# Block compression in two passes of fp32r, the causal mask moved into a scan, dummy transposes at the start, and a new plan of the order

## The chip, the core and the metric

One core of one Trainium2 chip runs the whole program. Its engines are PE (TensorE, matrix products), DVE (VectorE), ACT (ScalarE) and POOL (GpSimd); SP (SyncE) issues the transfers. The time is device microseconds of one execution, given as the median of several. A profile is one execution of its own.

## What is computed

One layer of a transformer on 1024 tokens of width 1024, in fp32. After a norm and an input projection, four mixers run: (a) attention over compressed blocks, over all keys and over a window of 512, gated; (b) a short convolution; (c) stick-breaking attention; (d) dilated attention. A norm by groups, the output projection, a second norm and a gated feed-forward block follow. The two pieces that the change touches:

```python
def compress_tokens(t, pe, w1, w2):        # for keys, then for values
    idx = jnp.arange(n_cmp)[:, None] * 16 + jnp.arange(32)[None, :]     # n_cmp = 63
    blocks = (t[:, idx] + pe).reshape(b, n_cmp, 32 * 64)
    return jax.nn.gelu(blocks @ w1) @ w2                                # 2048 -> 256 -> 64

def chunk(args):                           # stick-breaking attention, 4 heads
    z = jnp.einsum('bhqd,bhsd->bhqs', qi, k) * (hd ** -0.5)
    past = key_pos[None, :] < t[:, None]
    neg_log_keep = jnp.where(past, jax.nn.softplus(z), 0.0)
    between = lax.cumsum(neg_log_keep, axis=3, reverse=True) - neg_log_keep
    attn = jnp.where(past, jnp.exp(jax.nn.log_sigmoid(z) - between), 0.0)
```

## The kernel before

**Stages.** All of it is one function, `hybrid`. `x` is loaded in eight tiles of 128 tokens, normed, transposed on PE (`norm_transpose`, L189) and kept as a high and a low part in `XH`, `XL`. Most products are three PE passes over such pairs in the fp32r format (`mm3`, L234 to L236: high by high, high by low, low by high). Each weight tile of 256 KB is loaded into one of three buffers `raw` and split by `split` (L104 on ACT writes `whi`, L105 on POOL subtracts and writes `wlo`) into a ring of twelve buffers `whl`. First come the projections for mixer (a): `wA2` (268 columns), `kv` (the tokens to be compressed) and `wa` (the queries q, eight token tiles of 24 products each, called the q products below). Then the mixers run in the sequence of `ORDER`; then output projection and feed-forward, the larger part of the time, in which PE mostly sees one product of 512 columns after the other.

**The compression (L447 to L491).** It runs once for keys and once for values, z = 0 and 1. DVE adds the position term to the 63 overlapping blocks (L451, output `St`). `w1` comes in four loads of 512 KB straight into big buffers `St`, unsplit. For each of 16 positions and two halves of the 256 hidden units PE multiplies in plain fp32, with 63 moving columns (L459); the profile counts two records for each such product, 64 for each z. Then GELU is spelled out on ACT and DVE (L463 to L470, tiles `hT` and `ge`), a small weight `w2t` is loaded (L472) and PE makes the second product (L475). `hT`, `ge` and `w2t` come from the ring `S2` of ten buffers, of which the split q weights hold eight until the last q product; so `w2t` can be loaded only when `ge` has been read for the last time, at L470.

**The mask of (c).** `attn_stick` walks over pairs of query tiles. `qk_pair` makes two products per head (L501, L503); for the chunk with the diagonal a third product (L507) adds a tile `tri`, which holds -1e30 at and above the diagonal. ACT computes the softplus in three steps, DVE sums it from the right in a scan (L781, multiplier: a broadcast one), and `car` carries the sum to the next chunk (L786).

**What sets the order.** The program is traced twice. First `make_plan` lists every instruction with an estimated duration and lets each engine take the ready instruction of smallest index less lead; the table `LEADS` holds a lead for each engine and tile name, and rings hand out buffers in program order. The second time, `fix_order` pins every engine and SP to the order so found, up to the last product stage. Each engine then works through its list strictly in order, whatever waits.

Of the kernel before, what the change touches and what calls it, by code (L numbers as in the profile page):

```python
# [9 lines left out]
F32 = mybir.dt.float32  # L10
F32R = mybir.dt.float32r
# [13 lines left out]
WARM = 0  # L25
# [23 lines left out]
def hybrid(ctx, tc, pools, x, gmix, wa1, wa2, wkv, wcv, wd, wc, bgate, gcols, pe, w1, w2,  # L49
# [397 lines left out]
    for z, src in ((0, KK), (1, VV)):  # L447
        BL = Stile()
        bv = BL[:, :16 * 63].rearrange("p (l n) -> p l n", n=63)
# [12 lines left out]
        for j in range(2):  # L462
            nc.scalar.activation(hT[:, j * NBLK:(j + 1) * NBLK], ps[j][:, :NBLK], AF.Copy)  # L463
# [32 lines left out]
    def qk_pair(Q, K, qt, c0, n, diag=None, Z=None):  # L496
# [3 lines left out]
        for h in range(2):  # L500
            nc.tensor.matmul(ps[h][:, :n], Q[h][:, qc], K[h][:, kc_], start=True, stop=False)  # L501
            q2 = Q[h][:, qc] if Z is None else Z[:, h, :]
            nc.tensor.matmul(ps[h][:, :n], q2, K[2][:, kc_], start=False, stop=diag is None)  # L503
# [247 lines left out]
    def diag_mask():  # L751
        tri = sm.tile([128, 384], F32R, tag="wct", bufs=1, name="tri")
        t0 = S2("tri0")
        nc.gpsimd.memset(t0, 0.0)
        nc.gpsimd.affine_select(t0[:, 128:256], t0[:, 128:256], pattern=[[-1, 128]],
                                compare_op=OP.is_gt, fill=-BIG, base=0, channel_multiplier=1)
        nc.vector.tensor_copy(tri, t0[:, :384])
        return tri

    def attn_stick(hp, Q, K, V):  # L760
        for qp in range(NT // 2):
# [3 lines left out]
            for ci in range(qp // 2, -1, -1):  # L765
                for j in range(2):
# [4 lines left out]
                    ps = qk_pair(Q, K, qt, c0, max(256, w), w - 128 if diag else None, Z[j])  # L771
# [1053 lines left out]
```

## Time and profile before

| | us |
|---|---|
| median of 3 runs | 1329.57 (1325.78 to 1329.8) |
| the profiled execution's own time | 1334.16 |
| its span in the trace | 1332.4 |
| PE busy | 1297.2 (97% of the span) |
| DVE, ACT, POOL busy | 1025.5, 734.3, 597.9 |
| mean granted clock of PE over the recorded stretches | 0.988 |

The span is the time from the first to the last instruction; the rest of the execution's time lies around it. PE is the only engine that is nearly always busy, so a microsecond is gained where PE has less to do or waits less. A product's record is longer than the step from its start to the next one's start, because products are pipelined: costs are read from steps. The granted clock is the share of 2.4 GHz that PE was given in a stretch; 0.50 is 1.2 GHz.

### The profile page before, as it was taken

The page shows a single profiled execution, that of the slowest core. Times are in us where ns is not written, and L with a number is a line of the kernel's source. Part 1 is how long each engine was busy: PE and PEld are TensorE (multiplying, and loading weights), DVE is VectorE, ACT ScalarE, POOL GpSimd, SP SyncE. Part 2 cuts the span into 40 slices and gives each one's busy share as a digit, 9 for nine tenths or more (in the row PEclk, how much of TensorE's full clock was granted, in tenths as well). Part 3 has the DMA queues.
Part 4 walks back from the last instruction along what each step waited for, and adds up shares of the span by engine and source line. Part 5 has one row for each costly group of instructions (what it writes and reads, how often), then busy time and mean ns, then how long its engine had stood idle before and what let it go on. Part 6 is the DMA issues. An engine that isn't in the chain of part 4 may idle for free.

```text
span 1332.4 us, 20691 instructions
## 1 busy us (share of the span) xinstructions
PE 1297.2 (97%) x7101; PEld 1108.7 (83%) x7101; DVE 1025.5 (77%) x1985; ACT 734.3 (55%) x1643; POOL 597.9 (45%) x462
## 2 busy tenths in 40 slices
PE   6999999999999999899989999999999999999998
PEld 6898889989888878799968888888888887887886
DVE  5538889988896789788678898777775877499863
ACT  5427778877877888687655233323333335523440
POOL 4424356651312043433783445454443544464755
PEclk9989999999999999899999999999999999999999
DMA  6330012121312024424363544233232239762434
GB/s 223 129 113 1 9 45 72 41 64 26 104 49 58 15 68 144 152 84 139 128 217 135 182 161 163 96 119 119 87 111 79 87 119 328 266 200 76 141 92 155
DMA packets 89402, 153.07 MB, mean 115 GB/s; under 512 B 10001, under 2 KB 35601, under 8 KB 89297
## 3 DMA queue, kind: packets, MB, share of 16 engines
q1 hardware_dynamic: 88736, 149.92, 34.5%
q0 software_dynamic: 560, 1.84, 0.4%
q8 instruction: 56, 0.92, 0.3%
q14 instruction: 50, 0.40, 0.1%
HBM read 111.08 MB, written 36.44 MB: 111 GB/s over the span
## 4 chain that ended last, share of the span: by engine, by line
PE 85%; DVE 6%; DMA 3%; issue 2%; ACT 2%; POOL 1%; SPq 0%; DVEq 0%; POOLq 0%; ACTq 0%
PE PRp L234 10%; PE PRp L235 10%; PE PRp L236 10%; PE PRp L1048 4%; PE PRp L1047 4%; PE PRp L1046 4%; PE Op L568 3%; PE Op L569 3%; PE SPp L501 2%; PE Tp L1047 2%; PE SPp L1048 2%; PE SPp L1047 2%; PE Tp L1048 2%; PE SPp L1046 2%; PE Tp L1046 2%; PE SPp L503 2%
## 5 line engine op out<-in xcount | busy, mean ns | idle before, releaser
L105 POOL TENSOR_TENSOR wlo<-raw,whi 128x512 fp32r<-128x512 f32 x86 | 118.1, 1382 | 154.0 <-ACT whi L104 105.0
L1035 POOL TENSOR_TENSOR fw<-fraw,fw 128x512 fp32r<-128x512 f32 x50 | 72.9, 1458 | 139.2 <-ACT fw L1034 134.2
L541 DVE TENSOR_TENSOR ptl<-Tp,pth 128x256 fp32r<-128x256 f32 (+1 forms) x204 | 105.6, 534 | 25.3 <-ACT pth L540 23.5
L1105 DVE TENSOR_TENSOR fw<-sraw,fw 128x512 fp32r<-128x512 f32 x73 | 89.3, 1240 | 34.1 <-ACT fw L1104 33.9
L1034 ACT ACTIVATE fw<-fs 128x512 fp32r<-128x512 f32 x88 | 52.6, 629 | 113.5 <-DVE fs L1025 82.4
L540 ACT ACTIVATE pth<-Tp 128x256 fp32r<-128x256 f32 (+1 forms) x204 | 92.0, 471 | 33.9 <-PE Tp L562 25.3
L1105 POOL TENSOR_TENSOR hw<-bB,hw 128x512 fp32r<-128x512 f32 x55 | 80.0, 1467 | 49.6 <-ACT hw L1104 49.0
L234 PE MATMUL PRp<-XH,whi 128*128 128x512 f32 x224 | 90.5, 404 | 0.0
L236 PE MATMUL PRp<-XH,wlo 128*128 128x512 f32 x224 | 89.7, 400 | 0.0
L235 PE MATMUL PRp<-XL,whi 128*128 128x512 f32 x224 | 89.6, 400 | 0.0
L650 POOL TENSOR_SCALAR S<-S,ll 128x256 f32<-128x256 f32 (+3 forms) x48 | 60.2, 1260 | 54.2 <-DVE ll L647 26.9
L1035 DVE TENSOR_TENSOR fw<-fs,fw 128x512 fp32r<-128x512 f32 x88 | 76.7, 906 | 6.6 <-ACT fw L1034 6.6
L1034 ACT ACTIVATE fw<-fraw 128x512 fp32r<-128x512 f32 x50 | 31.4, 627 | 82.7 <-DMA fraw<-in_wup_dram 27.4
L236 PE MATMUL PRp<-whi,ML 128*128 128x256 f32 (+1 forms) x248 | 72.2, 295 | 2.3 <-DVE ML L814 2.3
L234 PE MATMUL PRp<-whi,MH 128*128 128x256 f32 (+1 forms) x248 | 72.6, 294 | 0.2 <-ACT MH L813 0.2
L235 PE MATMUL PRp<-wlo,MH 128*128 128x256 f32 (+1 forms) x248 | 72.2, 292 | 0.0
L1104 ACT ACTIVATE hw<-bB 128x512 fp32r<-128x512 f32 x62 | 38.9, 628 | 55.7 <-PE Op L236 20.4
L562 PE MATMUL Tp<-ident,S 128*128 128x128 f32 x292 | 68.1, 273 | 0.6 <-DVE S L748 0.4
L104 ACT ACTIVATE whi<-raw 128x512 fp32r<-128x512 f32 x86 | 53.0, 618 | 27.7 <-DMA raw<-in_wcv_dram 11.5
L560 PE MATMUL Tp<-ident,S 128*128 128x128 f32 x260 | 65.2, 272 | 0.0
L1104 ACT ACTIVATE fw<-sraw 128x512 fp32r<-128x512 f32 x73 | 45.3, 624 | 23.1 <-DMA sraw<-hS 13.5
L642 ACT ACTIVATE S<-S,mm 128x384 f32<-128x384 f32 (+3 forms) x96 | 55.7, 583 | 3.6 <-DVE mm L533 3.3
(469 smaller groups left out, 4619.8 us busy)
## 6 DMA issues: line engine op xcount, KB each, us to landing
fraw<-in_wgate_dram SPq DMA_DIRECT2D x22, 512.0 KB, 4.2
fraw<-in_wup_dram SPq DMA_DIRECT2D x22, 512.0 KB, 4.2
bB<-in_wdown_dram SPq DMA_DIRECT2D x44, 256.0 KB, 4.9
sraw<-hS SPq DMA_DIRECT2D x44, 256.0 KB, 2.7
raw<-in_wout_dram SPq DMA_DIRECT2D x30, 256.0 KB, 2.8
hS<-s SPq DMA_DIRECT2D x30, 256.0 KB, 2.2
sraw<-hA SPq DMA_DIRECT2D x29, 256.0 KB, 3.9
xt<-in_x_dram SPq DMA_DIRECT2D x8, 512.0 KB, 9.4
```

Of the source, the lines that this page charges most:

```text
L105: (lo or nc.gpsimd).tensor_tensor(dst_lo, raw, f(dst_hi), op=OP.subtract)
L234: nc.tensor.matmul(ps, a[0], b[0], start=first, stop=False)
L235: nc.tensor.matmul(ps, a[0], b[1], start=False, stop=False)
L236: nc.tensor.matmul(ps, a[1], b[0], start=False, stop=last)
L540: nc.scalar.activation(ph[:rows, c0:c1], tp[:rows, c0:c1], AF.Copy)
L541: nc.vector.tensor_tensor(pl[:rows, c0:c1], tp[:rows, c0:c1], f(ph[:rows, c0:c1]), op=OP.subtract)
L1035: eng.tensor_tensor(wt[:, 1, :], a, f(wt[:, 0, :]), op=OP.subtract)
L1046: nc.tensor.matmul(ps, wt[:, 0, c], bh[:, k, :], start=k == 0, stop=False)
L1047: nc.tensor.matmul(ps, wt[:, 0, c], bl[:, k, :], start=False, stop=False)
L1048: nc.tensor.matmul(ps, wt[:, 1, c], bh[:, k, :], start=False, stop=k == 3)
L1104: nc.scalar.activation(wt[:, 0, :], raw, AF.Copy)
L1105: eng.tensor_tensor(wt[:, 1, :], raw, f(wt[:, 0, :]), op=OP.subtract)
```

## The change

1. **Compression.** The blocks are split into a high and a low part side by side, `bhl` (128 columns: 63 high, a zero, 63 low, a zero), in a buffer of the ring `V`, which has two (the other holds `VA`, so `bhl` of z = 1 waits for the products of z = 0). `w1` comes in 16 loads of 256 KB through `raw` and `split`; the low part is subtracted on DVE for every other load. `bhl` becomes the stationary operand, and each position has two fp32r products of 256 columns (L464, L465): 64 in all, where 64 plain fp32 products with 128 records stood. Their result lies the other way round, so it is copied out (`hs`), transposed on PE (two transposes for each z) and the high and the low half are added on DVE before GELU.
2. **Mask.** The third product per head of the diagonal chunk (32 in all) goes. A tile `keep` of ones with a zero on the diagonal, in the ring `W`, is the scan's multiplier there, and the scan starts from 1e30 instead of 0: from the right it stays at 1e30 until the zero wipes it out. One carry in a special case is multiplied by a column of `keep`.
3. **Start.** `WARM = 32`: 32 transposes of the identity into an unused PSUM tile stand first in PE's list.
4. **Plan.** All numbers of `LEADS` are new, and with them the order on every engine up to the last stage.

```diff
-WARM = 0
+WARM = 32
...
-        ps = [SPt(), SPt()]
-        for l0 in range(0, 16, 4):
-            rw = Stile()
-            nc.sync.dma_start(rw.rearrange("p (l n) -> p l n", n=256), w1[z, :, l0:l0 + 4, :])
-            for l in range(4):
-                for j in range(2):
-                    c = l * 256 + j * 128
-                    nc.tensor.matmul(ps[j][:, :NBLK], rw[:, c:c + 128], bv[:, l0 + l, :],
-                                     start=(l0 + l == 0), stop=(l0 + l == 15))
+        bhl = sm.tile([128, 16, 2, 64], F32R, tag="V", bufs=2, name="bhl")
+        nc.gpsimd.memset(f(bhl[:, :, :, 63:64]), 0.0)
+        split(bhl[:, :, 0, 0:63], bhl[:, :, 1, 0:63], bv, lo=nc.vector)
+        ps = SPt()
+        for l0 in range(0, 16, 2):
+            raw = wraw()
+            nc.sync.dma_start(raw[:, :512].rearrange("p (l n) -> p l n", n=256), w1[z, :, l0:l0 + 2, :])
+            hi, lo = whl("whi"), whl("wlo")
+            split(hi[:, :512], lo[:, :512], raw[:, :512], lo=nc.vector if l0 % 4 else nc.gpsimd)
+            for l in range(2):
+                w = bhl[:, l0 + l, :, :]
+                c = slice(l * 256, (l + 1) * 256)
+                nc.tensor.matmul(ps[:, :256], w, hi[:, c], start=l0 + l == 0, stop=False)
+                nc.tensor.matmul(ps[:, :256], w, lo[:, c], start=False, stop=l0 + l == 15)
+        hs = S2("hs")
+        nc.scalar.activation(hs[:, :256], ps[:, :256], AF.Copy)
+        tp = Ttile()
+        for j in range(2):
+            nc.tensor.transpose(tp[:, j * 128:(j + 1) * 128], hs[:, j * 128:(j + 1) * 128], ident)
...
-        for j in range(2):
-            nc.scalar.activation(hT[:, j * NBLK:(j + 1) * NBLK], ps[j][:, :NBLK], AF.Copy)
+        nc.scalar.activation(hv, tv[:, :, 0, 0:NBLK], AF.Copy)
+        nc.vector.tensor_tensor(hv, tv[:, :, 1, 0:NBLK], hv, op=OP.add)
...
-        if diag is not None:
-            b = max(0, diag - 128)
-            for h in range(2):
-                nc.tensor.matmul(ps[h][:, b:b + 256], identr, tri_[0][:, b + 128 - diag:b + 384 - diag],
-                                 start=False, stop=True)
...
+        keep = sm.tile([128, T], F32, tag="W", bufs=2, name="keep")
+        nc.gpsimd.memset(keep, 1.0)
...
+                    mult = keep[:, 512 - w:512] if diag else one1.to_broadcast([128, w])
...
-                        nc.vector.tensor_tensor_scan(R[:, :w][:, ::-1], one1.to_broadcast([128, w]), S[:, ::-1],
-                                                     initial=0.0 if diag else car[h, j],
+                        nc.vector.tensor_tensor_scan(R[:, :w][:, ::-1], mult[:, ::-1], S[:, ::-1],
+                                                     initial=BIG if diag else car[h, j],
...
-    "SP S2 w2t": -307,
+    "SP S2 w2t": 98,
```

What the new plan moves is shown at three places, all in the compression. PE's list before, from the end of the first products (`SPp<-St`, z = 0) to the second ones (`SPp<-w2t,hT`); of the 61 q products (`PRp<-wa`) between them the first and the last are shown:

```order
L235 MATMUL PRp<-wa,XH 128x256
L459 MATMUL SPp<-St 128x63 x32
L236 MATMUL PRp<-wa,XL 128x256
...
L234 MATMUL PRp<-wa,XH 128x256
L475 MATMUL SPp<-w2t,hT 63x64 x2
L459 MATMUL SPp<-St 128x63 x20
```

PE's list now, from the last products of z = 0 (`SPp<-whi,bhl`) to the first ones of z = 1. Left out are q products, 4 in the first gap and 10 in the second:

```order
L464 MATMUL SPp<-whi,bhl 128x256
L465 MATMUL SPp<-wlo,bhl 128x256
L234 MATMUL PRp<-wa,XH 128x256
...
L236 MATMUL PRp<-wa,XL 128x256
L470 MATMUL Tp<-ident,hs 128x128 x2
L234 MATMUL PRp<-wa,XH 128x256
...
L236 MATMUL PRp<-wa,XL 128x256
L487 MATMUL SPp<-w2t,hT 63x64 x2
L464 MATMUL SPp<-whi,bhl 128x256
```

The second product of z = 0 still stands ahead of all products of z = 1, but 18 q products (6 and 12) and two transposes lie between it and the end of z = 0, where 61 q products lay. The 18 end a token tile: five of the eight tiles are then done.

DVE's list before, from the position terms (L451) to the end of GELU for z = 0 (L470):

```order
L451 TENSOR_TENSOR St<-St,pet 128x1008
L436 COPY St<-SPp 64x512
L451 TENSOR_TENSOR St<-St,pet 128x1008
L465 TENSOR_SCALAR ge<-ge 128x126
L466 TENSOR_TENSOR ge<-ge,hT 128x126
L468 TENSOR_SCALAR ge<-ge 128x126
L469 RECIPROCAL ge<-ge 128x126
L470 TENSOR_TENSOR hT<-hT,ge 128x126
```

The same stretch of DVE's list now, from the second position term on; `bhl<-St,bhl` is the subtraction for the low half of the blocks, `wlo<-raw,whi` a split of `w1`:

```order
L451 TENSOR_TENSOR St<-St,pet 128x1008
L105 TENSOR_TENSOR bhl<-St,bhl 128x16x63
L105 TENSOR_TENSOR wlo<-raw,whi 128x512 x3
L105 TENSOR_TENSOR bhl<-St,bhl 128x16x63
L105 TENSOR_TENSOR wlo<-raw,whi 128x512
L475 TENSOR_TENSOR hT<-Tp,hT 128x126
L477 TENSOR_SCALAR ge<-ge 128x126
L478 TENSOR_TENSOR ge<-ge,hT 128x126
L105 TENSOR_TENSOR wlo<-raw,whi 128x512
L480 TENSOR_SCALAR ge<-ge 128x126
L481 RECIPROCAL ge<-ge 128x126
L482 TENSOR_TENSOR hT<-hT,ge 128x126
```

The subtraction for z = 1 and two splits of its weights now stand between the end of the products of z = 0 and the end of GELU for z = 0.

SP's list, the difference in the compression (- before, + now):

```order
-L128 DMA raw<-in_wcv_dram 128x512 x2
-L455 DMA St<-in_w_dram 128x1024 x3
...
-L472 DMA w2t<-in_w_dram 128x128 x2
...
+L458 DMA raw<-in_w_dram 128x512 x15
+L484 DMA w2t<-in_w_dram 128x128
+L458 DMA raw<-in_w_dram 128x512
+L128 DMA raw<-in_wcv_dram 128x512 x6
+L484 DMA w2t<-in_w_dram 128x128
```

The loads of the convolution's weights `wcv` now follow all of `w1`, and the two small loads `w2t` stand behind 15 of the 16 loads of `w1` and behind all six of `wcv`. At the start of SP's list three small loads (`bgt`, `ind`, `pet`) now stand ahead of the first tile of `x`, where `pet` and `gcol` stood.

## Rows read from the trace of the kernel before

**Rows 1.** The page: busy time of each engine in us, its share of the span, number of instructions.

```profile
PE 1297.2 (97%) x7101; PEld 1108.7 (83%) x7101; DVE 1025.5 (77%) x1985; ACT 734.3 (55%) x1643; POOL 597.9 (45%) x462
```

**Rows 2.** The list of waits of PE over the whole span: who waited for whom, us in total, times, longest us.

```profile
PE Tp L189 <- DVE xn L178: 9.2, 1, 9.2
...
PE PRp L236 <- DVE ML L814: 2.3, 1, 2.3
PE SPp L459 <- DMA St<-in_w_dram: 1.8, 1, 1.8
```

**Rows 3.** The timeline of PE from the last q product ahead of the compression to the end of its products: start, length, what, count, idle time before it.

```profile
61.50 0.28 PE L235 MATMUL PRp<-wa,XH 128*128 128x256 f32 x1
63.62 11.65 PE L459 MATMUL SPp<-St 128*128 128x63 f32 x64 [1.84 <-DMA St<-in_w_dram]
75.03 0.56 PE L236 MATMUL PRp<-wa,XL 128*128 128x256 f32 x1
...
84.99 1.55 PE L459 MATMUL SPp<-St 128*128 128x63 f32 x12
...
90.04 0.27 PE L487 MATMUL Tp<-ident,kc 63*128 63x63 f32 x1
...
92.96 1.04 PE L339 MATMUL Tp<-ident,dup 128*128 128x128 f32 x8
```

**Rows 4.** Windows: stretch, its length, busy us of PE, weight loads, DVE, ACT, POOL, then the granted clock of PE, the DMA share and GB/s. The first two lie in the compression, the third at the change from the first to the second half of stick-breaking attention, the last in the feed-forward block.

```profile
63.60:75.10 11.50, 11.48 (x65) 11.50 (x65) 1.86 (x1) 1.94 (x4) 4.01 (x4) 0.61 0.88 308
75.10:79.90 4.80, 4.80 (x24) 4.80 (x24) 1.46 (x4) 2.33 (x7) 1.28 (x1) 0.51 0.78 255
...
538.90:554.30 15.40, 10.90 (x43) 9.00 (x44) 12.34 (x25) 7.89 (x18) 4.26 (x4) 0.67 0.67 211
...
680.50:684.00 3.50, 3.50 (x10) 2.72 (x9) 2.12 (x3) 1.69 (x4) 3.50 (x3) 0.51 0.67 243
```

**Rows 5.** The timeline of PE, q products of 256 columns: the first and the last of 21 in the slow stretch, then the first and the last of 46 in a row after it.

```profile
75.39 0.41 PE L234 MATMUL PRp<-wa,XH 128*128 128x256 f32 x1
...
79.65 0.36 PE L234 MATMUL PRp<-wa,XH 128*128 128x256 f32 x1
...
93.97 0.28 PE L236 MATMUL PRp<-wa,XL 128*128 128x256 f32 x1
...
99.36 0.28 PE L236 MATMUL PRp<-wa,XL 128*128 128x256 f32 x1
```

**Rows 6.** The mask tile `tri`: the products that add it, ns min/median/max, first and last start.

```profile
L507 PE MATMUL SPp<-tri,ident x32: 275/280/364, 415.5 to 601.7; 128*128 128x256 f32 x32
```

**Rows 7.** The timeline of ACT, DVE and SP for GELU of z = 0 and the load of `w2t`.

```profile
75.59 0.32 ACT L463 ACTIVATE hT<-SPp 128x63 f32<-128x63 f32 x2
...
77.15 0.29 DVE L466 TENSOR_TENSOR ge<-ge,hT 128x126 f32<-128x126 f32 x1
...
79.14 0.29 ACT L467 ACTIVATE ge<-ge 128x126 f32<-128x126 f32 x1
...
80.70 0.29 DVE L470 TENSOR_TENSOR hT<-hT,ge 128x126 f32<-128x126 f32 x1
...
81.02 0.33 SPq L472 DMA_DIRECT2D w2t<-in_w_dram  x1
```

**Rows 8.** The tile `w2t`: time from its load's issue to its landing.

```profile
DMA to landing us min/median/max: 1.7/2.2/2.6
```

**Rows 9.** The page's groups: the two halves of a weight split, count, busy us, mean ns of one, idle time before.

```profile
L105 POOL TENSOR_TENSOR wlo<-raw,whi 128x512 fp32r<-128x512 f32 x86 | 118.1, 1382 | 154.0 <-ACT whi L104 105.0
...
L104 ACT ACTIVATE whi<-raw 128x512 fp32r<-128x512 f32 x86 | 53.0, 618 | 27.7 <-DMA raw<-in_wcv_dram 11.5
```

**Rows 10.** Groups of DVE between 40 and 110 us: the addition over 1008 columns, and one of 512 columns from SBUF.

```profile
L451 DVE TENSOR_TENSOR St<-St,pet 128x1008 f32<-128x1008 f32 x2 | 3.8, 1904 | 3.4 <-PE SPp L459 3.4
...
L295 DVE TENSOR_TENSOR raw<-raw,hss 128x512 f32<-128x512 f32 x3 | 2.1, 693 | 3.8 <-POOL hss L95 3.8
```

**Rows 11.** The timeline of the first microseconds: two loads of SP, the identity on DVE, the first transposes of PE.

```profile
1.17 0.41 SPq L211 DMA_DIRECT2D gcol<-in_gcols_dram  x1
...
1.50 0.40 DVE L68 CAST ident<-idf 128x128 fp32r<-128x128 f32 x1
1.64 0.42 SPq L202 DMA_DIRECT2D xt<-in_x_dram  x1
...
9.20 1.94 PE L189 MATMUL Tp<-ident,xn 128*128 128x128 f32 x8 [9.20 <-DVE xn L178]
```

**Rows 12.** The timeline of PE: the first product after which it goes on without a break, eight transposes behind it, two products of 268 columns around the moment in which it first became fast, and eight transposes later.

```profile
12.92 0.59 PE L235 MATMUL PRp<-wlo,XH 128*128 128x268 f32 x1 [0.81 <-POOL wlo L105]
...
14.42 1.91 PE L189 MATMUL Tp<-ident,xn 128*128 128x128 f32 x8
...
18.14 0.40 PE L235 MATMUL PRp<-wlo,XH 128*128 128x268 f32 x1
...
18.50 0.29 PE L234 MATMUL PRp<-whi,XH 128*128 128x268 f32 x1
...
40.67 1.04 PE L189 MATMUL Tp<-ident,xn 128*128 128x128 f32 x8
```

**Rows 13.** DMA issues: count, KB each, median us from issue to landing.

```profile
St<-in_w_dram SPq DMA_DIRECT2D x8, 512.0 KB, 5.9
...
raw<-in_wd_dram SPq DMA_DIRECT2D x12, 256.0 KB, 2.8
```

More of the change, by code (lines that the diff above doesn't have):

```diff
@@ new lines @@
+    "ACT QK ckl": -144,
+    "ACT QK cqh": 97,
+    "ACT QK cql": -80,
+    "ACT QK dkh": -268,
+    "ACT QK dkl": -919,
+    "ACT QK dqh": 373,
+    "ACT QK dql": 71,
+    "ACT QK er": -549,
+    "ACT QK fw": 381,
+    "ACT QK ksh": 53,
+    "ACT QK kt": -64,
+    "ACT QK kwh": 453,
+    "ACT QK q01h": -746,
+    "ACT QK q01l": -329,
+    "ACT QK q23h": -826,
+    "ACT QK q23l": 31,
+    "ACT S2 S": -27,
+    "ACT S2 ge": 307,
+    "ACT S2 hT": 782,
+    "ACT S2 hs": 117,
+    "ACT S2 kv": 485,
@@ new lines @@
+    "ACT S2 wa": 171,
+    "ACT T3 T": -649,
+    "ACT T4 T": -539,
+    "ACT V VA": -104,
+    "ACT V VC": 61,
+    "ACT V VD": 152,
+    "ACT V bhl": 2,
+    "ACT V yc": 6,
+    "ACT X B": -146,
+    "ACT X MH": 45,
+    "ACT X T": 181,
+    "ACT X XH": -336,
+    "ACT gt gt": 76,
+    "ACT hss hss": 125,
+    "ACT kcT kcT": 249,
+    "ACT ll ll": -191,
+    "ACT otmp otmp": 527,
+    "ACT otmp tk": 191,
+    "ACT pth pth": -53,
+    "ACT pth sh": 6,
+    "ACT ss ss": -17,
+    "ACT tk raw": -571,
@@ new lines @@
+    "ACT tk rawk": 573,
+    "ACT tk sq": -338,
+    "ACT tk vraw": -177,
+    "ACT vcHL vcHL": 193,
+    "ACT whl c": 184,
+    "ACT whl p": -910,
+    "ACT whl sh": 328,
+    "ACT whl u": -617,
+    "ACT whl whi": -34,
+    "DVE B22 B": -57,
+    "DVE MO MO": -286,
+    "DVE QK St": -450,
+    "DVE QK ckr": 239,
+    "DVE QK cqh": -534,
+    "DVE QK cql": 219,
+    "DVE QK dkr": 424,
+    "DVE QK dqh": 249,
+    "DVE QK dql": -482,
+    "DVE QK er": -179,
+    "DVE QK fw": -1882,
+    "DVE QK ksl": 1174,
@@ new lines @@
+    "DVE QK kwl": -77,
+    "DVE QK q01h": -830,
+    "DVE QK q01l": 311,
+    "DVE QK q23h": -603,
+    "DVE QK q23l": -64,
+    "DVE QK x": 202,
+    "DVE S2 R": 440,
+    "DVE S2 ge": -70,
+    "DVE S2 hT": -130,
+    "DVE S2 kc": 137,
+    "DVE T4 T": -113,
+    "DVE V VA": 1653,
+    "DVE V VC": -140,
+    "DVE V VD": -237,
+    "DVE V bhl": -123,
+    "DVE V yc": 203,
+    "DVE W xn": -849,
+    "DVE X ML": 309,
+    "DVE X T": -1190,
+    "DVE X XL": -252,
+    "DVE blk1r blk1r": -484,
+    "DVE car car": -9,
@@ new lines @@
+    "DVE df df": -75,
+    "DVE df fs": -715,
+    "DVE epst epst": -764,
+    "DVE gates gates": -762,
+    "DVE gsc gsc": 3,
+    "DVE gt gt": -22,
+    "DVE half half": 1535,
+    "DVE hss hss": -377,
+    "DVE ident ident": -251,
+    "DVE ll ll": 15,
+    "DVE mm mm": 1,
+    "DVE nt nt": 751,
+    "DVE one1 one": -1358,
+    "DVE pad0 Sc": 56,
+    "DVE pad1 Sc": 5,
+    "DVE pth pth": -9,
+    "DVE ptl ptl": 9,
+    "DVE rsqm rsqm": 1,
+    "DVE ss ss": -360,
+    "DVE ssm ssm": 114,
+    "DVE tk dup": 85,
@@ new lines @@
+    "DVE tk raw": 129,
+    "DVE vcHL vcHL": 140,
+    "DVE whl c": -37,
+    "DVE whl p": -382,
+    "DVE whl s": 180,
+    "DVE whl u": 1080,
+    "DVE whl wlo": 92,
+    "PE SP SPp": 170,
+    "POOL QK fw": -395,
+    "POOL S2 S": 143,
+    "POOL S2 kv": 370,
+    "POOL S2 wa": 710,
+    "POOL T3 T": 709,
+    "POOL V bhl": 418,
+    "POOL W keep": 322,
+    "POOL X B": 529,
+    "POOL X MH": -27,
+    "POOL X T": 414,
+    "POOL hss hss": -433,
+    "POOL pad0 Sc": -636,
+    "POOL pad0 zq": 544,
@@ new lines @@
+    "POOL pad1 Sc": -409,
+    "POOL pad1 zq": 82,
+    "POOL ptl sl": 335,
+    "POOL ss ss": -75,
+    "POOL vcHL vcHL": -1039,
+    "POOL whl idf": 1178,
+    "POOL whl p": 752,
+    "POOL whl s": -181,
+    "POOL whl sl": 926,
+    "POOL whl u": -687,
+    "POOL whl wlo": -68,
+    "SP QK ckh": -394,
+    "SP QK ckl": 713,
+    "SP QK dkh": -392,
+    "SP QK dkl": 90,
+    "SP QK fraw": 93,
+    "SP QK gbc": 55,
+    "SP QK gm": 35,
+    "SP QK x": -978,
+    "SP QK xt": 3,
+    "SP S2 kvr": -50,
```

222 lines of the change are left out of this document (41 added, 181 removed).

## The prediction

> **What bounds the kernel.** I read the page's busy times first [rows 1]: PE works 97% of the span, so the question is only how much work PE loses and where it waits. PE's list of waits [rows 2] says that little waiting is left: 9.2 us ahead of the first transposes, 2.3 us for a gain, 1.8 us for a load of `w1`. So I looked for time that PE spends busy but slow. The timeline shows it in the compression [rows 3]: 64 records of 63 columns take 11.4 us the first time and under 8 us the second. The windows give the reason [rows 4]: the granted clock was 0.61 and 0.51 there, half of 2.4 GHz for most of it. It fell after the 2 us without work at 61.5, under narrow products; it was full again at 79.8, after 4.8 us of products of 256 columns. The steps of those show both levels [rows 5]: 20 steps from 75.39 to 79.65 are 213 ns each, 45 steps from 93.97 to 99.36 are 120 ns. Elsewhere PE is at its floor, and a change can pay only by taking PE's work, its waits or its slow stretches away.
>
> **The compression, what goes.** From the starts in [rows 3]: the gap 61.50 to 63.62 less one step of 0.12, 2.0 us; the first 64 records, 63.62 to 75.03, 11.4 us; the q products behind them at 213 instead of 120 ns, 20 steps and the first one, 2.1 us; the second 64 records, 84.99 to 92.96 less the transpose of 0.2, 7.8 us. Together 23.3 us. **What comes:** 64 products of 256 columns at 120 ns, 7.7 us, and four transposes at 0.11 us (eight take 1.04 with their tail [rows 12]), 0.4 us. If PE always had its operands, the stage would lose 23.3 - 8.1 = 15.2 us.
>
> **What takes it back.** The products now need split operands. ACT gains 16 splits of 0.62 us and POOL eight of 1.4 [rows 9], DVE eight of 0.7 and two over 1008 columns, at most 1.9 each [rows 10]. By count they fit beside 192 q products (23 us of PE). Not by order. After the last product of z = 0, PE's list holds 18 q products and two transposes, 18 x 0.12 + 0.22 = 2.4 us, and then the second product, with all of z = 1 queued behind it. That product needs GELU and `w2t`, and `w2t` is issued when GELU is done: before, `hT` was copied at 75.59, the last GELU step ended at 80.99, and the load went out at 81.02 [rows 7]. It then takes 2.2 us [rows 8]. Before, 61 q products covered this, and PE did not wait. Now the chain from the end of z = 0 is: GELU's 5.4 us as measured; less 1.7 us in which its exponential stood behind other work of ACT (77.44 to 79.14); plus the copy `hs`, its transposes and the addition of the halves, about 1.4 us with their handovers (copies of that width took 0.3, two transposes 0.22). That is 5.1 us if nothing is in the way. DVE's list puts the subtraction over 1008 columns (1.1 to 1.9 us) and two splits (0.7 each) ahead of its end, so up to 3 us more. With the load: 7.4 to 10.4 us against 2.4 us of cover. PE would stand 5 to 8 us; I take 7, since the DVE list has all three in the way. More q products cannot fill it: the 18 finish the fifth token tile, three PSUM banks hold the unread ones, and the copy that frees one stands later in ACT's list.
>
> Behind a wait of that length the clock should be half, as it was after 2.0 us at 61.5. It came back after 3.4 us of dense products at 680.5 [rows 4] and stayed low for 13 us in the compression. Half of such a stretch is lost: 1.7 to 6.8 us; I take 2.2, because the products behind the wait are dense. For the first products of z = 0, whose `bhl` waits for two additions of 1.9 us on DVE, and for single late splits, I add 0.5 us (0 to 2). The compression nets -15.2 + 7.0 + 2.2 + 0.5 = **-5.5 us** (-15.2 to +1.6).
>
> **The mask.** 32 products of 256 columns go [rows 6], 32 x 0.12 = -3.8 us, as PE is the bound there too; 0 if ACT and DVE set the pace. The scan reads a second SBUF tile instead of a broadcast; both are one operand of the same length, so I price that at nothing, hidden under PE. `keep` needs a buffer of `W` after the last use by the dilated mixer; some ten DVE instructions lie between that use and the first scan, enough for three short POOL steps. **-3.8 us** (-3.8 to 0).
>
> **The start.** The identity is ready at 1.90, so 32 transposes, 0.21 us each at half clock (eight took 1.94 with their tail [rows 11], against 1.04 later [rows 12]), run from 2.05 to 8.9 us, just under the first real ones at 9.20. From 12.92 to some 18.4 us PE works without a break at half speed [rows 12]: transposes at 0.21 us, products with records of 0.40 us until 18.14 and of 0.29 from 18.50. At full clock these 5.5 us of work would take half, a gain of up to 2.7 us; but after its first transposes PE has next to nothing to do until 12.92, so the clock may fall again. The first load of `x` moves behind one more small load, 0.47 us (1.17 to 1.64 [rows 11]). I take half of the gain: -1.35 + 0.45 = **-0.9 us** (-2.2 to +0.5).
>
> **The plan.** The new order touches every wait up to the last stage. Before, the worst place outside the compression is 538.9 to 554.3, where PE was busy 10.9 of 15.4 us at a clock of 0.67 [rows 4]; such places can go or come. Their size gives +-6 us around 0.
>
> **The sum.** -5.5 - 3.8 - 0.9 = -10.2 us. The profiled execution of 1334.16 us would be 1324.0. It lies 4.6 us above the median of the runs; carried over to that, 1329.57 - 10.2 = 1319.4, so I predict **1319 us**.
>
> **Rivals.**
> *PE does not stand before the second product.* If GELU's engines are free when it needs them, or the pieces of z = 0 come so late that its q products shift behind it, the waits and the slow stretch (9.2 us) shrink to nothing: 1310 us. For it: the stage's 31 us of PE work exceed what the split engines have to do. Against it: the load of `w2t` follows GELU in the trace, and the lists leave 2.4 us. Chance 0.22.
> *The dummy transposes do nothing.* In the trace, eight transposes at 14.42 stand in the slow stretch [rows 12], and nothing shows whether they helped to end it. Then the start costs 0.45 instead of gaining 0.9: 1320.7 us. Chance 0.5, whatever the rest does; it moves no sign. The Trainium skill, "TensorE: Matmul & The Clock Gate", Part 4: PE-mode transpose, says that transposes do not engage the full clock as products do. By that rule this rival is the case, and the sum is -8.9 us; the trace shows real transposes at both levels, so it leaves the rule open.
> *The plan eats the gain.* A second place like 538.9 appears, with 4.5 us of idle PE and some 5 us at half clock: 1329 us, no change. For it: the lists leave PE little to fill with where the halves of the stick-breaking attention meet, as before. Against it: that place exists already and is in the time. Chance 0.13.
> *The load ring starves what follows; slower.* `w1` now passes through three buffers, 22 loads with the convolution's six behind them, about seven turns, and the second `w2t` stands behind all. A turn is a landing of 2.8 us [rows 13] and two splits. If landings take the 5.9 us that `w1` had before [rows 13], each turn is 3.1 us longer, 22 us in all. The 72 q products left then are 8.6 us, of which GELU's chain takes 5, so some 4 us are covered: 1319 + 18 = 1337 us. It ends slower by over 0.3% once a turn grows by about 2.6 us (the 10 us of the forecast, 4 more and the cover of 4, in seven turns). Against it: the old 512 KB loads came three at a time with others, the new ones wait for each other. Chance 0.06.
>
> **How the numbers follow.** The forecast has 0.59: 1313 to 1325 with its terms. With the rival at 1310 and most of the one at 1329 the range is 1307 to 1328; outside lie the load ring, both early gains at once with a better plan, and a plan still worse. About 0.3%, 4 us, is what a measurement here can tell from no change: faster than 1325.6 in the forecast nearly always and in the first rival, 0.82; within 0.12; slower 0.06.
>
> **What would show it.** Right: a wait of PE of 5 to 8 us ahead of the product with `w2t`, near 76 us, a granted clock of 0.5 just behind it, no L507, and 64 records of 256 columns at steps of 120 ns where the clock is full. Wrong: no such wait, so that z = 1 follows z = 0 within 3 us (first rival); a wait named after a load of `wcv` or after the second `w2t` (the ring). Records of 0.29 us for 268 columns before 13 us would speak for the transposes. Waits of several us or a clock below full between 100 and 680 us would mean that the plan decides, and that my reading of one place was too narrow.

## The result and the profile after

| | before | after |
|---|---|---|
| median | 1329.68 us (4 runs, 1325.78 to 1335.0) | 1344.43 us (4 runs, 1342.64 to 1348.91) |
| ratio to before, 95% interval | | 1.0113 (1.007 to 1.0156) |
| the profiled execution's own time, its span | 1334.16, 1332.4 | 1344.89, 1343.2 |

The kernel became 1.1% slower; the forecast was 0.8% faster. The medians lie 14.8 us apart and the two profiled executions 10.8, because that of the kernel before lies 4.5 us above its median; the traces below account for the 10.8. The page's first line, engine by engine as in [rows 1], shows nothing of it: PE is busy 1.4 us less than before, in a span that is 10.8 us longer.

```profile
PE 1295.8 (96%) x7041; PEld 1100.0 (82%) x7041; DVE 1021.6 (76%) x1996; ACT 750.1 (56%) x1661; POOL 610.8 (45%) x473
```

PE's list of waits over the whole span (who waited for whom, us in total, times, longest), to be read beside [rows 2]:

```profile
PE SPp L487 <- DMA w2t<-in_w_dram: 7.0, 1, 7.0
PE Tp L606 <- ACT sh L605: 3.0, 2, 2.3
PE PRp L236 <- DVE ML L827: 2.9, 1, 2.9
PE Op L576 <- DVE ptl L548: 2.8, 6, 1.2
PE PRp L366 <- ACT vraw L363: 2.3, 3, 0.9
PE SPp L234 <- ACT kv L104: 2.1, 1, 2.1
```

The first is the wait that was forecast, to the microsecond. The other five are the next in the list: `kv` lies ahead of the compression, the rest among the attention mixers. With the lines not shown, PE's waits between the first score product of (a) and the last attention transposes add up to 19.3 us, against 10.6 before.

The timeline of PE in the compression, for [rows 3]: the first product of z = 0, the wait, the first and the last slow product of z = 1, the transposes behind it.

```profile
70.61 0.36 PE L464 MATMUL SPp<-whi,bhl 128*128 128x256 f32 x1 [0.69 <-DVE bhl L105]
...
87.98 0.66 PE L487 MATMUL SPp<-w2t,hT 128*63 128x64 f32 x4 [7.00 <-DMA w2t<-in_w_dram]
88.57 0.58 PE L464 MATMUL SPp<-whi,bhl 128*128 128x256 f32 x1
...
94.07 0.39 PE L465 MATMUL SPp<-wlo,bhl 128*128 128x256 f32 x1
...
96.62 0.44 PE L470 MATMUL Tp<-ident,hs 128*128 128x128 f32 x2
```

From 88.95 to 94.07 z = 1 goes in 24 steps of 0.213 us, then at 0.12. The windows for [rows 4] (stretch, length, busy us of PE, weight loads, DVE, ACT, POOL, granted clock, DMA share, GB/s): the wait, z = 1, a place in the dilated mixer, and the change between the two halves of stick-breaking attention.

```profile
80.80:88.00 7.20, 0.20 (x3) 0.05 (x1) 5.19 (x11) 3.14 (x6) 2.55 (x2) 0.73 0.50 159
88.00:96.60 8.60, 8.60 (x48) 8.30 (x48) 4.23 (x7) 3.03 (x8) 5.15 (x4) 0.63 0.47 150
361.00:371.00 10.00, 7.75 (x44) 6.58 (x43) 6.79 (x15) 5.05 (x10) 1.27 (x1) 0.83 0.23 70
548.00:572.30 24.30, 16.31 (x66) 13.20 (x66) 20.43 (x43) 15.57 (x37) 5.00 (x4) 0.58 0.43 145
```

The last is the bad place of before ([rows 4], 538.9 to 554.3, PE busy 10.9 of 15.4 us): it now lasts 24 us, of which PE works 16.3, at a clock of 0.58. The one at 361 is new.

**Where the time went.** For every record of a product in a trace I took the step to the next one's start and subtracted the median step of that shape at full clock in the kernel before (0.058 us for 63 or 64 columns, 0.109 for a transpose, 0.12 for 256, 0.124 for 268, 0.175 for 384, 0.232 for 512). What is left, where it is above zero, is what PE lost to waits and to the half clock; the dummy transposes and the time ahead of the first product are left out. Summed over three stretches, in us, for the one profiled execution of each kernel; the ratio is that of all runs to runs of the kernel before made beside them, whose median lay between 1327.6 and 1330.9 us:

| kernel | median us | ratio to before | lost ahead of the first score product of (a) | lost from there to the last attention transposes | lost behind |
|---|---|---|---|---|---|
| before | 1329.7 |  | 23.6 | 53.2 | 18.0 |
| after | 1344.4 | 1.0113 | 23.3 | 70.1 | 15.7 |
| mask_alone | 1337.4 | 1.0065 | 24.2 | 53.7 | 22.7 |
| compression_alone | 1337.5 | 1.0061 | 20.6 | 59.4 | 18.4 |
| new_code_old_numbers | 1336.2 | 1.0049 | 19.1 | 61.3 | 21.3 |
| old_code_new_numbers | 1355.6 | 1.0197 | 31.8 | 66.3 | 21.8 |
| old_code_table_shaken | 1353.8 | 1.0181 | 27.2 | 65.5 | 21.4 |
| mask_old_order | 1328.3 | 0.9986 | 22.6 | 53.3 | 17.2 |
| transposes_alone | 1328.2 | 0.9979 | 25.5 | 53.5 | 13.6 |
| mask_and_transposes_old_order | 1325.0 | 0.9956 | 25.1 | 53.2 | 14.5 |
| compression_old_order | 1344.8 | 1.0111 | 36.3 | 51.3 | 15.3 |
| both_old_order | 1340.5 | 1.0083 | 36.8 | 51.8 | 16.1 |
| new_order_to_110_old_behind | 1336.3 | 1.0048 | 25.8 | 58.7 | 15.1 |
| second_product_late | 1346.2 | 1.0111 | 26.6 | 68.6 | 15.3 |
| big_loads | 1340.1 | 1.0090 | 21.9 | 69.2 | 13.1 |
| big_loads_second_late | 1343.6 | 1.0107 | 23.7 | 68.0 | 12.8 |
| all_edits_fitted_order | 1322.1 | 0.9936 | 24.4 | 50.5 | 13.8 |
| mask_transposes_fitted_order | 1326.2 | 0.9971 | 23.2 | 48.8 | 15.3 |

The kernel after lost 16.9 us more than before in the attention, where the forecast had the plan at 0 with +-6, and gained nothing ahead of it.

### The profile page after: what moved, and what is told of

The parts are those of the page before. It is cut to its first block, busy times and chain, and to the rows that moved or that the text cites. A ratio compares the mean times of both kernels' runs of the same rounds, so it can differ in the third digit from the quotient of the medians.

```text
span 1343.2 us, 20626 instructions
## 1 busy us (share of the span) xinstructions
PE 1295.8 (96%) x7041; PEld 1100.0 (82%) x7041; DVE 1021.6 (76%) x1996; ACT 750.1 (56%) x1661; POOL 610.8 (45%) x473
## 4 chain that ended last, share of the span: by engine, by line
PE 81%; DVE 9%; ACT 3%; issue 3%; DMA 2%; POOL 1%; SPq 0%; DVEq 0%; ACTq 0%; POOLq 0%
PE PRp L234 10%; PE PRp L235 9%; PE PRp L236 9%; PE PRp L1061 4%; PE PRp L1060 3%; PE PRp L1059 3%; PE Op L575 3%; PE SPp L513 2%; PE Op L576 2%; PE SPp L1061 2%; PE SPp L1059 2%; PE SPp L1060 2%; PE Tp L1061 2%; PE Tp L1059 2%; PE Tp L1060 2%
## 5 line engine op out<-in xcount | busy, mean ns | idle before, releaser
L105 POOL TENSOR_TENSOR wlo<-raw,whi 128x512 fp32r<-128x512 f32 x94 | 132.1, 1415 | 145.8 <-ACT whi L104 95.1
L548 DVE TENSOR_TENSOR ptl<-Tp,pth 128x256 fp32r<-128x256 f32 (+1 forms) x204 | 105.9, 531 | 25.8 <-ACT pth L547 23.5
L1048 DVE TENSOR_TENSOR fw<-fs,fw 128x512 fp32r<-128x512 f32 x88 | 73.3, 867 | 11.1 <-ACT fw L1047 11.0
L104 ACT ACTIVATE whi<-raw 128x512 fp32r<-128x512 f32 x102 | 62.8, 619 | 33.3 <-PE PRp L235 11.9
L569 PE MATMUL Tp<-ident,S 128*128 128x128 f32 x292 | 70.5, 279 | 0.0
L567 PE MATMUL Tp<-ident,S 128*128 128x128 f32 x260 | 67.1, 279 | 0.6 <-ACT tk L610 0.6
L1038 DVE TENSOR_TENSOR fs<-fraw 128x512 f32<-128x512 f32 x44 | 41.8, 950 | 30.8 <-DMA fraw<-in_wup_dram 16.8
```

The source lines that it names most:

```text
L105: (lo or nc.gpsimd).tensor_tensor(dst_lo, raw, f(dst_hi), op=OP.subtract)
L548: nc.vector.tensor_tensor(pl[:rows, c0:c1], tp[:rows, c0:c1], f(ph[:rows, c0:c1]), op=OP.subtract)
L1048: eng.tensor_tensor(wt[:, 1, :], a, f(wt[:, 0, :]), op=OP.subtract)
```

## The experiments

Three theories at the start: the new table of numbers is simply worse (T); a table fits only the code for which it was made (F); the edits themselves cost the time (E).

**Tables and code crossed.** `new_code_old_numbers` puts the old numbers into the changed code, `old_code_new_numbers` the new ones into the old code; the diff is the table alone.

> The changed kernel with the 146 numbers of LEADS that the kernel before had (all other edits stay). From 120 to 680 us the changed kernel's PE lost some 18 us more beyond its floor than before. Theory T (the new table is simply a worse one): most of that comes back, 1326 to 1331 us. Rival F (each table fits only the code for which it was made; any other pairing of code and table leaves PE short of operands in many places): no better than the changed kernel, 1338 to 1350 us. Rival E (the edits themselves cost the time, whatever the order): 1342 to 1346 us, with the same gaps as in the changed kernel.

> The kernel before with the 150 numbers of the changed kernel's LEADS, nothing else. T (a worse table): slower by the 13 to 18 us that the changed kernel lost between 120 and 680 us, 1342 to 1348 us. F (no table fits foreign code): slower too, 1338 to 1350 us. E (the edits cost it): 1326 to 1334 us, as before.

Measured 1336.19 us, 1.0049 (1.0032 to 1.0066), and 1355.61 us, 1.0197 (1.0177 to 1.0217). The first lies in none of the three ranges, the second above all of them. Half of the loss comes back with the old table, so the new one is worse even for its own code (T, in part); on the old code it costs 26 us, so E falls; and the old table on the new code is still slower than before (F, in part).

**Each edit alone, old table.**

```diff
-                nc.tensor.matmul(ps[h][:, b:b + 256], identr, tri_[0][:, b + 128 - diag:b + 384 - diag],
-                                 start=False, stop=True)
...
+                    mult = keep[:, 512 - w:512] if diag else one1.to_broadcast([128, w])
```

> The kernel before with the mask edit alone (no third product, scan with the tile of ones and a zero), numbers of before. T: the 32 products go and nothing else happens, 1325 to 1327 us. F: the order is planned anew with numbers that no longer fit, 1335 to 1350 us, with waits of PE also far from the stick-breaking attention. E: slower only between 410 and 630 us, where the scans run; 1335 to 1342 us.

> The kernel before with the compression edit alone, numbers of before. T: the compression as measured in the changed kernel is worth about -1 us with its wait of 7 us ahead of the second product, and nothing else happens: 1327 to 1331 us. F: 1335 to 1350 us, with new waits of PE behind 120 us. E: the loss is in the first 120 us, 1335 us or more.

For the compression the diff is its part of the change. Measured 1337.43 us, 1.0065 (1.0045 to 1.0085), and 1337.48 us, 1.0061 (1.0045 to 1.0077). F for both: E's times fit too, but not the places where it puts the loss. For the compression the table has 20.6 us ahead of the attention, less than before. For the mask the largest new wait is

```profile
PE Tp L908 <- DVE nt L178: 5.0, 3, 3.5
```

and that is the second norm, behind the mixers, which the mask does not touch: the rows of PE's list that the new plan moved reach from 429 to 862 us.

**The old order shaken.** The same code, each number moved up or down by 5 at random.

```diff
-    "ACT B22 B": 12,
-    "ACT QK St": -322,
+    "ACT B22 B": 7,
+    "ACT QK St": -327,
...
```

> The kernel before, each of its 146 numbers moved up or down by 5 at random, nothing else; about 1200 of 6100 rows of PE's order ahead of the last stage move. Theory F (the old table was fitted to its code, and any other order nearby loses): 1334 to 1345 us, with waits of PE that the kernel before does not have. Rival S (most orders are as good): 1327 to 1333 us.

Measured 1353.78 us, 1.0181 (1.0155 to 1.0207): 24 us for an order that nothing asked for. That is more than F's range; S falls. Behind the first transposes, the largest of PE's waits are these; the list of the kernel before has the second with 0.6 us and the other two not at all:

```profile
PE Tp L907 <- DVE nt L178: 4.3, 3, 3.1
PE SPp L501 <- DVE S L787: 3.3, 1, 3.3
PE PRp L234 <- DVE dql L308: 2.9, 1, 2.9
```

So the size of the term "plan" was to be had from the old kernel itself: a neighbour of the old table, the only one measured, costs 1.8%. That the old table was fitted to its code agrees with this, and no run shows how it was made.

**Edits with the order held.** The kernel traces the unedited program first, plans it, and gives each instruction of the edited one the place of its counterpart; only the edit's own rows move. A new instruction stands where what it needs is done by the old plan.

```diff
-    start, slots = make_plan(tc, pools)
+    old, first, tags = _traced(_program(tc))
+    begun = _planned(old, first, tags)[0]
...
+    start, slots = follow_plan(tc, pools, old, begun)
```

> The mask edit alone, with the order of the kernel before kept row for row on every engine (the 32 products with the mask tile are gone; the three POOL steps that make the tile of ones stand where the two for the old tile stood; the product of one carry stands where its copy stood). Theory O (an edit is worth what it removes while the order is held, and the new plan is what costs): 32 x 0.12 = 3.8 us less, 1325.5 to 1327.5 us. Rival E (the edit itself costs, by the scan with a second tile or the wait for its buffer): about 1337 us, as with the plan made anew. Rival N (PE's work is not the bound there): 1329 to 1331 us.

> The compression edit alone, with the order of the kernel before kept for all else: 61 q products stay between the products of z = 0 and the second product, where the new plan leaves 18. O: no wait ahead of the product with w2t, 10 to 15 us less than before, 1315 to 1321 us, and nothing new behind 110 us. E (the splits or the loads of w1 hold PE up): 1327 us or more, with waits for splits of w1 or of the convolution's weights. Rival G (the chain of GELU is the limit whatever stands between): the wait of some 7 us stays, 1324 to 1329 us.

> Compression and mask edits together (no dummy transposes), the order of the kernel before kept for all else. O: the two gains add, 1311 to 1317 us. E: 1330 us or more. N for the mask: 1315 to 1321 us.

Mask: 1328.32 us, 0.9986 (0.9969 to 1.0002). Beside the 1.0065 with a new plan, E is out for the mask; by time, O and N both lie in the interval. The traces decide between them, at the first score product of (a) and the last attention transposes, before and with the mask edit (the last two numbers ahead of the semicolon are the first and the last start, in us):

```profile
L682 PE MATMUL SPp<-kcT,q01h x16: 216/272/323, 106.4 to 171.0; 128*128 128x63 f32 x16
L602 PE MATMUL Tp<-sl,blk1r x24: 276/282/415, 133.0 to 637.6; 128*128 128x256 f32 x24
...
L729 PE MATMUL SPp<-kcT,q01h x16: 216/273/322, 104.7 to 169.3; 128*128 128x63 f32 x16
L649 PE MATMUL Tp<-sl,blk1r x24: 274/281/415, 131.2 to 632.1; 128*128 128x256 f32 x24
```

The stretch takes 531.2 us before and 527.4 with the edit, 3.8 less, at the same loss (53.2 and 53.3): O, in this pair of executions. Compression: 1344.76 us, 1.0111 (1.0091 to 1.0131); both: 1340.46 us, 1.0083 (1.006 to 1.0106). By time E holds for both, and O and G fall: with the compression alone the wait for `w2t` is 0.8 us. But PE's two largest waits there, behind the first transposes, are not for the splits or loads of `w1` that E names:

```profile
PE Tp L500 <- ACT hs L497: 6.6, 2, 4.1
PE SPp L492 <- DVE bhl L108: 4.9, 1, 4.9
```

The new handovers have no good place in the old order; the loss lies ahead of the first score products (36.3 us, and the first of them starts at 119.1 us where it was 106.4), none behind them (51.3).

**Dummy transposes alone** (`WARM = 32` in the kernel before, all other rows in their order).

> The kernel before with the 32 dummy transposes ahead of all else, and the same order otherwise. Theory U (they raise the clock at once, but PE then waits for data until about 13 us and the clock falls back under the first products): 1329 to 1331 us, as before, with a granted clock of 1.0 from about 6 us, 0.5 again for several us behind the first products. Rival V (the clock, once up, stays up): 1327 to 1328 us, records of 268 columns at 0.29 us from the first one on.

Measured 1328.19 us, 0.9979 (0.9965 to 0.9994). U has the clock right, but by time a gain is there, near V's range. The windows of its first microseconds, columns as above:

```profile
12.40:15.80 3.40, 3.33 (x15) 3.33 (x16) 1.26 (x3) 1.27 (x3) 2.79 (x3) 0.50 1.02 410
15.80:18.40 2.60, 2.60 (x22) 2.46 (x22) 2.05 (x3) 2.47 (x5) 0.70 (x1) 1.00 1.02 401
```

The clock is full again from 15.8 us; before, records got short at 18.50 [rows 12], and in `mask_old_order`, which starts with the same rows and has no dummy transposes, at 16.96. In the kernel after it was full only from 19.2.

The traces do not show the gain at the start. The first score product of (a) starts later with the transposes than without: here at 107.4 us against 106.4 in the kernel before, and in the next experiment at 107.3 against 104.7 in `mask_old_order` (both lines without them stand above).

```profile
L682 PE MATMUL SPp<-kcT,q01h x16: 216/273/323, 107.4 to 172.0; 128*128 128x63 f32 x16
L729 PE MATMUL SPp<-kcT,q01h x16: 216/273/322, 107.3 to 171.9; 128*128 128x63 f32 x16
```

Near 21 us the same row of PE starts 1.0 us earlier than before (0.4 of it already at the first product), and 0.1 us earlier in the second pair; that is lost again in the compression, where the clock fell earlier and stayed low longer. Windows of the half clock there, before and with the transposes, then of a place in the feed-forward block, before and with the transposes:

```profile
66.20:79.80 13.60, 13.60 (x65) 13.60 (x65) 2.69 (x5) 4.27 (x10) 5.04 (x4) 0.50 0.83 275
63.60:80.60 17.00, 17.00 (x82) 17.00 (x81) 2.99 (x4) 4.26 (x10) 6.09 (x4) 0.50 0.74 252
...
1228.00:1236.00 8.00, 6.89 (x23) 5.27 (x23) 8.00 (x6) 4.02 (x8) 8.00 (x5) 0.79 0.19 60
1225.00:1233.00 8.00, 7.16 (x31) 5.49 (x30) 8.00 (x7) 4.92 (x9) 6.72 (x5) 1.00 0.20 67
```

This execution is ahead of that of before only by what it did not lose behind the mixers (13.6 us against 18.0), in code and order that are the same. Why the runs with the transposes are faster stays open.

**Mask and transposes together, order of before.**

> The two edits that did no harm by themselves, mask and dummy transposes, in the order of the kernel before; compression and table as before. If the two add: 1.3 us and 2.2 to 2.8 us below the kernel before, 1325 to 1327 us. If the earlier start of the first products is swallowed by the next wait: 1328 to 1330 us.

Measured 1325.01 us, 0.9956 (0.994 to 0.9971): by time the two add (0.9986 x 0.9979 = 0.9965).

**The wait ahead of the second product taken away**, in the changed kernel's own order.

```diff
+        if SECOND_LATE and z == 1:
+            second(*held)
         hs = S2("hs")
...
-        second(z, hT, w2t)
+        if z == 0:
+            held = (z, hT, w2t)
+        else:
+            second(z, hT, w2t)
```

> The changed kernel, its own order kept row for row, but the second product of z = 0 (and the few steps that follow from it) stands behind the 32 products of z = 1 instead of ahead of them. Theory W (the wait of 7.0 us is paid because z = 1 is queued behind the product with w2t): the wait shrinks to under 1 us and the half-speed stretch behind it goes, 7 to 10 us less than the changed kernel, 1334 to 1338 us. Rival R (the operands of z = 1 are late as well): the wait moves to the products of z = 1, at most 2 us less, 1342 to 1345 us. Rival K (the keys are then late for the attention that waits for them): up to 4 us less, with a wait ahead of the first score products near 110 us, 1340 to 1342 us.

Measured 1346.15 us, 1.0111 (1.0094 to 1.0128). W and K fall; R holds, 1 us above its range: the wait of 7 us is gone and nothing comes back. PE's timeline, first products of z = 1 with waits:

```profile
80.77 0.35 PE L493 MATMUL SPp<-whi,bhl 128*128 128x256 f32 x1 [0.37 <-DVE bhl L109]
...
82.53 0.38 PE L494 MATMUL SPp<-wlo,bhl 128*128 128x256 f32 x1 [0.46 <-POOL wlo L109]
...
86.16 0.58 PE L494 MATMUL SPp<-wlo,bhl 128*128 128x256 f32 x1 [1.07 <-POOL wlo L109]
...
91.36 0.69 PE L457 MATMUL SPp<-w2t,hT 128*63 128x64 f32 x4
```

32 products that are worth 3.8 us take from 80.77 to 91.36; records of 0.28 us become 0.41 on the way, so the half clock came as well. ACT, which splits `w1`, waits in this kernel for its loads, and so it does in the changed kernel. From its list of waits between 66 and 96 us, in this kernel and in the changed one:

```profile
ACT whi L108 <- DMA raw<-in_w_dram: 9.9, 11, 2.2
ACT whi L104 <- DMA raw<-in_w_dram: 8.4, 8, 2.5
```

**Is it the loads?** In the changed kernel the 16 loads of `w1` go out from 59.1 to 86.8 us, each when one of three buffers is free. Here they come as eight loads of 512 KB into the big buffers, as before, with PE's order held.

```diff
-            raw = wraw()
-            nc.sync.dma_start(raw[:, :512].rearrange("p (l n) -> p l n", n=256), w1[z, :, l0:l0 + 2, :])
+            if l0 % 4 == 0:
+                rw = Stile()
+                nc.sync.dma_start(rw.rearrange("p (l n) -> p l n", n=256), w1[z, :, l0:l0 + 4, :])
+            raw = rw[:, l0 % 4 * 256:l0 % 4 * 256 + 512]
```

> The changed kernel in its own order (PE's list unchanged), but w1 comes in eight loads of 512 KB into the big buffers, as in the kernel before, and is split from there; the 16 loads of 256 KB through three buffers, issued from 59.1 to 86.8 us, are gone. Theory S (those loads are what holds the pieces of z = 1 up): the pieces are split by 84 us, the wait of 7 us ahead of the product with w2t stays (its place in PE's list is the same), and z = 1 runs without gaps behind it; 1 to 3 us less than the changed kernel, 1341 to 1344 us. Rival X (the engines that split, and the order of their lists, hold them up): no change, 1343 to 1347 us.

> The same, and the second product of z = 0 behind the products of z = 1. S: no wait ahead of the second product, no waits for pieces of w1, 6 to 10 us less than the changed kernel, 1334 to 1339 us. X: as with the late second product alone, waits for pieces of z = 1 and a granted clock of 0.5 behind 84 us, 1343 to 1347 us.

Measured 1340.09 us, 1.009 (1.007 to 1.011), and 1343.64 us, 1.0107 (1.009 to 1.0124). The first interval overlaps the changed kernel's 1.0113 (1.007 to 1.0156), so a small gain from the loads is neither shown nor excluded (1.009 of 1329.68 us is 1341.6, in the range of S); the second says X. ACT's timeline in that second kernel:

```profile
72.30 0.63 ACT L108 ACTIVATE whi<-St 128x512 fp32r<-128x512 f32 x1 [0.53 <-DMA St<-in_w_dram]
77.67 1.05 ACT L108 ACTIVATE bhl<-St 128x1008 fp32r<-128x1008 f32 x1 [4.74 <-PE SPp L500]
78.62 0.36 ACT L504 ACTIVATE hs<-SPp 128x256 f32<-128x256 f32 x1
```

ACT stands 4.7 us in front of `bhl` of z = 1, whose buffer is free only after the last product of z = 0, and the splits of z = 1 are queued behind it. They then come one after the other between the steps of GELU. So the loads did hold ACT up, and once they are early, the next thing does.

**Which part of the order?** The changed kernel with its own order to about 110 us (PE's first 545 rows) and the order of before behind it.

> The changed kernel (all edits), with its own order through the compression (PE's list is the same for its first 545 rows, to about 110 us) and with the order of the kernel before behind that. Theory L (the loss of the changed kernel lies in the new order behind 120 us, some 15 us net of the mask): it comes back, 1327 to 1332 us, with the wait of 7 us ahead of the product with w2t still there. Rival M (what the compression hands on late upsets any order behind it): 1335 us or more, with waits between 120 and 300 us beyond those of the kernel before.

Measured 1336.28 us, 1.0048 (1.003 to 1.0065). M by time, but between L and M in what it says: 8 of the 14.8 us come back (1344.43 - 1336.28). The attention loses 58.7 us, 11.4 less than in the changed kernel and 5.5 more than before.

**An order fitted to the changed code.** All edits, the second product late, the order of before as a priority, with a shift for each engine and tile name, chosen anew by the planner's own estimate. Beside it the same search without the compression edit.

```diff
+    key = [k - SHIFT.get(o.group, 0) for k, o in zip(key, ops)]
     start, slot = _follow(ops, first, tags, key)
```

> All edits, the second product of z = 0 behind the products of z = 1, and a third order: it follows the order of the kernel before as a priority, with shifts per engine and tile name chosen anew for the changed code. Theory P (the loss is one of order, and the compression can pay under a fitting one): 1318 to 1326 us, with no more lost between 110 and 640 us than in the kernel before. Rival Q (the compression's chain is longer whatever the order, and what waits for its keys is late): 1330 us or more, with new waits between 100 and 300 us.

> Mask and dummy transposes without the compression edit, with an order found in the same way. If the same way of finding an order helps here as well: 1318 to 1324 us; if the order of the kernel before cannot be bettered so: 1325 to 1335 us.

Measured 1322.08 us, 0.9936 (0.992 to 0.9952), and 1326.21 us, 0.9971 (0.9957 to 0.9985). P holds, Q falls. The second lies where its text puts an order that cannot be bettered: for mask and transposes the search gained nothing (0.9956 in the order of before). The windows of the fitted kernel at z = 1, behind it, and at the change between the two halves of stick-breaking attention:

```profile
79.00:87.00 8.00, 5.34 (x28) 4.22 (x26) 6.38 (x12) 3.83 (x8) 3.72 (x3) 0.84 0.53 171
87.00:95.00 8.00, 8.00 (x52) 7.76 (x52) 3.37 (x6) 4.06 (x10) 6.87 (x6) 0.73 0.52 166
535.00:550.00 15.00, 11.45 (x62) 9.79 (x63) 12.62 (x26) 9.11 (x21) 5.29 (x5) 0.77 0.67 231
```

The compression is no better there than in the changed kernel (24.4 us lost ahead of the first score products, against 23.3). What is gone are 20 us in the attention: 50.5 against 70.1. It has the lowest median of this study. What the compression edit itself is worth under a fitting order is shown only narrowly: the interval lies just below that of the fitted order without it, but overlaps that of mask and transposes in the order of before (0.9956), and the profiled executions of the two fitted kernels have spans of 1320.8 and 1320.4 us.

## Why the prediction was wrong

**The step that failed is "The plan": "their size gives +-6 us around 0".** It sized a new order by the worst place in one trace, and centred it on no change. The attention lost 16.9 us more. The sign that the prediction itself names for this came: a clock below full between 100 and 680 us, 0.83 at 361 and 0.58 for 24 us from 548, with waits of up to 2.9 us. That it is the order is shown three times on the same edits: the old numbers give 8 us back, the old order behind 110 us gives the same 8, and a fitted order, with the second product late, gives 22 (1344.4 to 1322.1), where the second product late gave nothing by itself. The rival "the plan eats the gain" had the mechanism, even the place, and a price of 10 us (1329 instead of 1319) where 16.9 was due. The reading of [rows 2] helped to miss it: it names three waits, and the line left out between them is one of 2.8 us in five places of the attention (`PE Op L568 <- ACT pth L540: 2.8, 5, 0.9`).

In these single executions, 11.4 of the 16.9 us go when the order of before stands behind 110 us, and 5.5 stay with the new order ahead of it. Late keys alone do not cost the attention: in `compression_old_order` the first score product comes 12.7 us later than before and the attention loses no more (51.3). Which rows of the new order cost the 11.4 us is not shown.

**The compression, -5.5, came out 2.4 us short, inside its range.** Between 56 and 112 us PE lost 17.6 us before and 13.8 after, -3.8; the new products and transposes are 0.7 us more work than the old ones (64 x 0.12 + 4 x 0.109 against 128 x 0.058), so the stage nets -3.1. The wait was 7.0 us where 7 was taken, though from 81.0 us on and not near 76; behind it, 24 steps lost 0.093 each, 2.2 us, as taken; the late pieces of z = 0 cost 0.69 and some 0.6 us, together 1.3, where 0.5 was taken. Wrong was what hung on it: that without the wait the stage would be worth 15.2. "If PE always had its operands" is the premise of that number and of the first rival (1310), and no order tried here meets it. In the changed kernel ACT waits 8.4 us for the loads of `w1`; with the loads early it stands 4.74 us in front of `bhl` of z = 1, which shares a ring with z = 0, and its split blocks the others. The Trainium skill, "PSUM — Partial Sum Buffer", section "Engine vs sequencer instructions", calls the queues of ScalarE, VectorE and GpSimdE strictly first in, first out; the splits that stand behind `bhl` in these 4.74 us agree. The prediction went through the lists of PE and DVE at this place, but not through the splits in ACT's.

**The load ring.** Its loads go out over 27.7 us and hold ACT up, but they were not what decided: with eight large loads the ratio is 1.009 against 1.0113, with intervals that overlap.

**The mask, -3.8 (-3.8 to 0).** L507 is gone; with the order held the gain is 0.14% of 1329.7, 1.9 us (4.1 to -0.3). By time both ends are still inside; the traces show the 3.8 in the attention, as PE's 527.4 against 531.2 us. The scan's second tile was rightly priced at nothing: with the order held, 256 columns take 738 ns on average, against 736.

**The start, -0.9 (-2.2 to +0.5).** By itself 0.21%, 2.8 us (0.8 to 4.7): by time larger than taken, but not shown where the term puts it, as the first score product comes 1.0 and 2.6 us later with them. The rival that the transposes do nothing falls by time for the kernel before and is not decided by the traces; in the changed kernel full clock came only at 19.2 us.

**The sum.** -3.1 in the compression, +2.1 for `kv` ahead of it and some 1 us of small losses there, -3.8 for the mask, +16.9 in the attention and -2.3 behind it make some +11; the spans differ by 10.8.

## What to carry to other kernels

Where a table of numbers fixes the order, an edit is two changes: hold the order to price the edit, and price a new order by what a neighbour of the old one costs (here 1.8%, one neighbour), not by the worst place in the trace. A wait that the profile names is worth only as much as the work queued behind it is ready; read the lists of the engines that feed it before counting it as gain. Edits that lose under one order can win under another: the same ones gave 1.0113 and, with one product moved, 0.9936. A gain in time that the trace does not show at the place of the edit, like that of the transposes here, is not yet explained.

## What the runs showed of the hardware

Transposes alone brought the clock up. Two windows of the kernel after, the first half and the second half of the 32 dummy transposes, ahead of which PE had done nothing, and one from 12.4 us on:

```profile
2.00:5.50 3.50, 3.49 (x17) 3.49 (x18) 0.00 (x0) 0.08 (x1) 0.00 (x0) 1.00 0.64 151
5.50:7.50 2.00, 1.93 (x17) 1.69 (x15) 0.00 (x0) 1.05 (x2) 0.00 (x0) 1.00 0.95 336
...
12.40:19.20 6.80, 6.17 (x28) 6.17 (x29) 4.11 (x6) 4.55 (x9) 4.31 (x4) 0.50 1.03 405
```

The steps between their starts are 0.213 us up to the start at 5.48 us and 0.109 from that at 5.63 us on (no clock is recorded ahead of 5.55 us; the first window's 1.00 stands for nothing). The Trainium skill, "TensorE: Matmul & The Clock Gate", Part 4: PE-mode transpose, says that transposes do not engage the full clock; this trace shows that these did. PE then worked 1.6 of the 5 us to 12.4, and the clock was half from there to 19.2, under the first products.
